# Moving a small weight preparation to GpSimd and its queue, and two requests to a later place

## The chip, the cores and the metric

The kernel runs on one core of one Trainium2 chip. A core has five engines that run their own instruction streams: TensorE (PE in the profile; its weight loads are PEld), VectorE (DVE), ScalarE (ACT), GpSimd (POOL) and SyncE (SP). All wait for one another by semaphores. Transfers between DRAM and the on-chip memory are requested by an engine and carried out by 16 DMA engines; a request from SP or ScalarE goes to a hardware queue of that engine, a request from GpSimd to a queue whose descriptors GpSimd writes. An engine issues its instructions in order, so an instruction that waits holds everything behind it on that engine.

The metric is the device time of one execution in microseconds, and the profile's span is the time from its first to its last instruction.

## The reference

Two independent sequences of 512 tokens and 1024 features go through the same two layers. All arithmetic is in float32; the kernel splits each operand into a high and a low part and multiplies these.

```python
def fourier_mix(h, w_out):
    B, S, _ = h.shape
    hg = h.astype(jnp.float32).reshape(B, S, N_FGROUPS, F_GROUP)
    f = jnp.fft.fft2(hg, axes=(1, 3), norm="ortho").real
    f = f.reshape(B, S, D_MODEL).astype(h.dtype)
    return f @ w_out

def trunk(x, ...):
    for i in range(DEPTH):
        j = i // N_MIXERS
        if i % N_MIXERS == 0:
            x = x + fourier_mix(rms_norm(x, fourier_norm[j]), fourier_w_out[j])
        else:
            x = x + gqa_attention(rms_norm(x, attn_norm[j]), ...)
        x = x + sq_relu_mlp(rms_norm(x, mlp_norm[i]), mlp_w_up[i], mlp_w_down[i])
    return rms_norm(x, final_norm)
```

Only the first operation, the Fourier mixing of layer 0, is touched by the change. The features fall into 8 groups of 128; the real part of a transform over 512 tokens and 128 features is taken per group, and the result is multiplied by the 1024x1024 matrix `w_out`.

## The kernel before, in words

**The work in order.** The kernel does the Fourier mixing of sequence 0 and then of sequence 1, then the first MLP for both, the attention, and the second MLP. The change lies in the first 60 us, in the mixing.

**The Fourier stage.** The real transform is symmetric, so each sequence is folded first: tokens are halved by sums and differences, and features too. `Front(q, c)` makes the folded inputs of sequence `q`, half `c`: squares for the norm (L124), the gain (L381), the difference `minus` (L394), the sum `plus` (L385) or, for sequence 1, `plus_there` (L390, an accumulating DMA from GpSimd), the norm's scale (L405, L411) and `combine` (L419 to L436). `transform(q, mid, hook)` multiplies by the token tables and then by the feature tables; for sequence 0 it uses exact tables (`exact`), for sequence 1 the tables `dcos`, `dsin`, `dalt` and `dfeat` (loaded by `table`, L309). `mid` and `hook0` are pieces of work that `transform` places between its products.

**The output weights.** `w_out` is folded as well. `Fold(j)`, for four row blocks, loads two halves from `w_four` on SP (L318, L319), takes their difference on VectorE (`minus`, L616) and their sum by an accumulating DMA that GpSimd issues (L617), and then splits both into high and low parts: `odd` from the difference, `even_hi` (L626, ScalarE) and `even_lo` (L630, VectorE) from the sum. `odd_outs` multiplies by the differences, for all eight output blocks at once, so that it holds all eight banks of the accumulator; `odd_put` (L696, L697) empties a bank on ScalarE into the output tile `xs[0, i]`. `even_outs` multiplies by the sums, one output block at a time, over four row blocks.

**The half-range rows.** Each feature group has one frequency, the 64th, that the folding does not cover. Its weight rows are eight differences of rows of `w_out`, and they enter as one more product at the end of each `even_outs` (L673): the weight tile there has 72 partitions, in which rows 0 to 7 and 64 to 71 hold the high part and rows 32 to 39 the low part. `FoldNyq` prepares this. `load` brings the raw rows (64 KB, from `w_nyq`), spread over 128 partitions; `combine` takes a difference on VectorE (L647) and its rounded copy on ScalarE (L648); `put` takes the low part on VectorE (L652), stores both parts to a DRAM tile called `nyq` (L653) and reads them back in the layout of the 72 partitions (L655, three loads). The store and the loads are requested by SP. The loads wait for the store's landing.

**What sets the order.** Up to the end of this stage, the program order of every engine is written out by hand (`manual_schedule` with all five engines). In later stages TensorE's order is written by hand and that of most other work is chosen by a planner, from planned times. Tiles named `u` come from one pool of 38 buffers; a new tile takes a buffer that is free by then, and its first write waits for whatever last used the buffer.

The order around the change, before: SP requests the inputs of sequence 0 and the exact tables, then the norms' columns `gc` (L333), the weights of `Fold(0)` and `Fold(1)`, the raw half-range rows (L643), the weights of `Fold(2)` and `Fold(3)`, and the four inputs of sequence 1 (L299), then the store and the three loads of `nyq`. GpSimd issues the four weight sums, the two `plus_there` of sequence 1's first half, the four tables, a small multiply (L401) and a memset (L425) of `g0`'s `combine`, and then the two `plus_there` of the second half. `gc` is first read by `blocks.gain` (L206), in the MLP's preparation.

Of the kernel before, what the change touches and what calls it, by code (L numbers as in the profile page):

```python
# [12 lines left out]
F32 = mybir.dt.float32  # L13
# [6 lines left out]
P = 128  # L20
# [4 lines left out]
KC = D // P  # L25
# [19 lines left out]
def trunk_kernel(ctx, tc, x_in, xt_in, y_out, tables, rope, gfour, gcol, grow, gfin,  # L45
                 w_four, w_nyq, w_qkv, w_o, w_a22, w_up, w_row2, w_row4, w_sum2, w_sum4, w_down):
    nc = tc.nc
    ctx.enter_context(nc.allow_low_precision(reason="operands split into float32r halves"))

    cons = ctx.enter_context(tc.tile_pool(name="cons", bufs=1))  # L50
# [10 lines left out]
    def nm(s):  # L61
        n_[0] += 1
        return f"{s}_{n_[0]}"

    def slot(shape, dt):
        return act.tile(shape, dt, tag="u4", name=nm("u"))
# [7 lines left out]
    def ps():  # L74
        return psp.tile([P, 512], F32, tag="ps", name=nm("ps"))

    def f32(ap):
        return ap.bitcast(F32)
# [116 lines left out]
    class Blocks:  # L195
# [25 lines left out]
        def put(self, name, f):  # L221
            h = slot([P, 2, 512], F32R), slot([P, 2, 512], F32R)
            split(h[0], h[1], f)
            self.b.setdefault(name, []).append(h)
# [82 lines left out]
    def table(k):  # L307
        tabs[k] = slot([P, D], F32R)
        nc.gpsimd.dma_start(tabs[k][:, : tables[k].shape[-1]], tables[k])  # L309
# [12 lines left out]
    def begin():  # L322
        gr = slot([P, D], F32)
        nc.sync.dma_start(gr, gfour)
        load_x(0, 0, nc.scalar)
        load_x(0, 1)
        exact_table(4)
        for t in range(2, 4):
            load_x(0, t)
        exact_table(5)  # L330
        exact_table(6)
        gc = cons.tile([P, 4 * KC], F32, name="gc")
        nc.sync.dma_start(gc, gcol)  # L333
        return gr, gc

    one = small(1)
    nc.vector.memset(one[:, :1], 1.0)
# [206 lines left out]
    def idle(o, n):  # L544

        for _ in range(n):
            nc.tensor.matmul(o[:, :256], filler, filler.unsqueeze(1).broadcast_to([P, 2, P]), start=True, stop=True)
# [85 lines left out]
    class FoldNyq:  # L633
# [7 lines left out]
        def load(self):  # L641
            self.h = slot([P, 4, 64], F32R)
            nc.sync.dma_start(f32(self.h[:, 2:]), w_nyq)  # L643

        def combine(self):
            h, ab = self.h, f32(self.h[:, 2:])
            nc.vector.tensor_sub(ab[:, 0], ab[:, 0], ab[:, 1])  # L647
            nc.scalar.copy(h[:, 0], ab[:, 0])  # L648

        def put(self):  # L650
            h, ab = self.h, f32(self.h[:, 2:])
            nc.vector.tensor_sub(h[:, 1], ab[:, 0], f32(h[:, 0]))  # L652
            nc.sync.dma_start(self.d.rearrange("i a (b f) -> (a b) i f", b=16), f32(h[:, :2]))  # L653
            for r, i in ((0, 0), (32, 1), (64, 0)):
                nc.sync.dma_start(f32(self.w[r : r + 8]), self.d[i])  # L655

# [20 lines left out]
    def odd_outs(q, fos):  # L679
        return outs(q, fos, wo, 256, 256)  # L680
# [26 lines left out]

    ET = mybir.EngineType
    with tc.manual_schedule(engines={ET.PE, ET.Activation, ET.DVE, ET.Pool, ET.SP}):
        gr, gc = begin()  # L710
        nc.scalar.activation(one[:, :1], one[:, :1], AF.Sqrt)
        cosX = [exact[0][:, :258], exact[0][:, 514:772], exact[1][:, 256:514]]
        sinX = [exact[0][:, 258:514], exact[1][:, :256], exact[1][:, 514:770]]
        ftX, pickX = exact[2][:, :256], exact[2][:, 256:334]
        f0, f1, wn = Front(0, 0), Front(0, 1), FoldNyq()
        idle(ps(), 61)
        f0.squares(0)
        f0.gain(0)
        f0.minus(0)
        f0.plus(0)  # L720
        f0.squares(1)
        f0.gain(1)
        f0.chain(0, 6)
        f1.squares(0)
        f0.minus(1)
        f0.plus(1)
        f0.scale_both(0)
        f1.gain(0)
        f1.squares(1)
        f1.chain(1, 2)  # L730
        f0.scale_both(1)
        f1.minus(0)
        f1.gain(1)
        fold = [Fold(j) for j in range(2)]
        wn.load()

        def mid():
            f1.chain(0, 1)
            f1.plus(0)
            f1.chain(2, 6)  # L740
            f1.scale()
            f1.minus(1)
            f1.plus(1)
            f1.combine()
            put_nyq()
            wn.combine()
            fold[0].minus()
            fold.append(Fold(2))
            fold.append(Fold(3))
            for t in range(NT):  # L750
                load_x(1, t)
            wn.put()
        g0, g1 = [Front(1, c) for c in range(2)]

        def hook0(at, j):
            if at == "seq":
                if j == 0:
                    fold[1].minus()
                    fold[0].odd()
                elif j == 2:  # L760
                    fold[2].minus()
                    fold[1].odd()
                elif j == 3:
                    fold[3].minus()
                    fold[2].odd()
            elif j == 3:
                fold[3].odd()
                g0.squares(0)
                g0.gain(0)
                g0.minus(0)  # L770
                g0.plus_there(0)
                g0.squares(1)
                g0.gain(1)
                g0.minus(1)
                g0.plus_there(1)
                for k in range(4):
                    table(k)

        transform(0, mid, hook0)
        for i in range(4):  # L780
            xs[0, i] = slot([P, 2, 512], F32)
        o = odd_outs(0, range(KC))
        g0.chain(0, 2)
        fold[0].even_hi()
        fold[1].even_hi()
        g0.chain(2, 6)
        fold[0].even_lo()
        fold[1].even_lo()
        g0.scale(slice(0, 1))
        fold[2].even_hi()  # L790
        fold[2].even_lo()
        odd_put(0, 0, o[0])
        fold[3].even_hi()
        fold[3].even_lo()
        for fo in range(1, 4):
            odd_put(0, fo, o[fo])
        g0.scale(slice(1, 2))
        g1.gain(0)
        for fo in range(4, 6):
            odd_put(0, fo, o[fo])  # L800
        g0.combine()
        for fo in range(6, 8):
            odd_put(0, fo, o[fo])
        g1.minus(0)
        g1.plus_there(0)
        g0.split_even()
        g1.gain(1)
        g0.split_odd()

        def even(fo):  # L810
            even_put(0, fo, even_outs(0, [fo])[0])
            if fo % 2:
                add_input(0, fo // 2)

        g1.squares(0)
        even(0)
        g1.minus(1)
        g1.plus_there(1)
        g1.squares(1)
        even(1)  # L820
        even(2)
        g1.chain(0, 2)
        even(3)
        g1.chain(2, 6)
        even(4)
        g1.scale(slice(0, 1))
        even(5)
        g1.scale(slice(1, 2))
        even(6)
        g1.combine()  # L830
        g1.split_hi()
        even(7)
        g1.split_lo()

        put_away(0, 2)
        load_xs(1, xt_in[1])
        raws = [load_raw(w_up[0, 2 * p]) for p in range(4)]
        blocks = Blocks(0)

        def hook1(at, j):  # L840
            if at == "seq":
                if j < 3:
                    square(0, j)
            else:
                square(0, 3 + j)
                if j == 3:
                    square(0, 7)

        transform(1, hook=hook1)
        for fo in range(KC):  # L850
            e, = even_outs(1, [fo])
            even_add(1, fo, e)
            if fo < 4:
                for i in range(2 * fo, 2 * fo + 2):
                    blocks.gain(0, i)
                if fo != 2:
                    put_away(0, fo)
            if fo == 2:
                blocks.root(0)
            if fo == 3:  # L860
                blocks.spread(0)
            if 3 < fo:
                blocks.first(fo - 4)
            if 5 < fo:
                blocks.first_lo(fo - 6)
        rows = []

        def gain1(fo):
            blocks.gain(1, fo)
            if fo % 2:  # L870
                put_away(1, fo // 2)

        for fo in range(KC):
            odd_add(1, fo, odd_outs(1, [fo])[0])
            if fo == 7:
                rows.append(halves(raws[3]))
            if fo:
                square(1, fo - 1)
            if fo > 1:
                gain1(fo - 2)  # L880
            if fo < 2:
                rows.append(halves(raws[fo]))
            if 1 < fo < 4:
                blocks.first_lo(fo)
            if fo == 5:
                rows.append(halves(raws[2]))
        square(1, KC - 1)
        for fo in range(KC - 2, KC):
            gain1(fo)
# [494 lines left out]
    for which, sc in (("q", HD ** -0.5), ("k", 1.0)):  # L1384
        r = slot([P, 2, NT, HD], F32)
# [319 lines left out]
    with tc.manual_schedule(engines={ET.PE}):  # L1705
# [14 lines left out]
        for k, name in enumerate(("t2", "t3", "t4")):  # L1720
            h = heads_out.operand(name)
# [334 lines left out]
```

## Time and profile before

| | us |
|---|---|
| median of 3 runs | 1689.15 |
| the three runs | 1680.93, 1689.15, 1689.36 |
| the profiled execution | 1683.1 |
| its span | 1681.3 |
| TensorE busy in the span | 1664.4 |
| VectorE, ScalarE, GpSimd busy | 1259.3, 873.4, 385.3 |

How to read the rows that follow. A row of the timeline is: start, length, engine, line of the kernel, operation, tile written and tile read with their shapes, how many, and in brackets the idle time of the engine just before and what ended it. A row of a wait list is: engine and tile, the line that waited, who ended the wait, then total time, how often, longest. A row of the chain is start, length and what; the chain is followed backwards from the end of the kernel, at each step to the event that released it. A row of the DMA list is: tile written and read, the engine that issued, how many, KB of each, and the time from the request to the landing. A row of a stretch gives its busy time per engine, the clock granted to TensorE, the mean share of the 16 DMA engines and the rate. The name `ps` is an accumulator bank, `w` and `raw` are weight buffers.

### The profile page before, as it was taken

Reading aid. Unit: us, or ns where it says so; the run is one execution under the profiler, and the core shown is the slowest. Engines: PE = TensorE matmul, PEld = TensorE weight load, DVE = VectorE, ACT = ScalarE, POOL = GpSimd, SP = SyncE. Lnnn points to the kernel's source line nnn. Section 1 sums busy time; section 2 is a strip of 40 time slices with the busy share of each in tenths; the row PEclk is TensorE's granted clock in tenths of the full one; section 3 lists DMA queues with packets and bytes.
Section 4 is the critical chain, followed back from the end, with each engine's and each line's share of the span. In section 5 each row is a group of like instructions: output and inputs, shape, how many; then the busy total and the mean of one; then the engine's idle time right before and its main releaser. Section 6 shows DMA issues by size and latency. Waiting matters only on the chain.

```text
span 1681.3 us, 22281 instructions
## 1 busy us (share of the span) xinstructions
PE 1664.4 (99%) x7845; PEld 1386.3 (82%) x7845; DVE 1259.3 (75%) x1850; ACT 873.4 (52%) x1538; POOL 385.3 (23%) x357
## 2 busy tenths in 40 slices
PE   9999999999999999999999999999999999999998
PEld 8988888888888888788878888888888888888887
DVE  7779786557886869869888877777855487878865
ACT  6766454446342435446698854554544553433334
POOL 2321443221000001324544303004422220000002
PEclk9999999999999999999999999999999999999999
DMA  9842655449775757425501146334644696757532
GB/s 319 249 154 94 208 188 193 157 163 368 257 225 165 247 173 228 169 76 187 177 1 39 63 164 224 124 114 162 213 152 156 225 371 196 235 157 233 180 102 100
DMA packets 122239, 302.99 MB, mean 180 GB/s; under 512 B 12408, under 2 KB 13560, under 8 KB 122128
## 3 DMA queue, kind: packets, MB, share of 16 engines
q1 hardware_dynamic: 98896, 254.21, 43.5%
q0 software_dynamic: 8832, 20.89, 5.8%
q10 hardware_dynamic: 14400, 26.48, 4.2%
q8 instruction: 61, 1.00, 0.2%
q14 instruction: 50, 0.41, 0.1%
HBM read 218.11 MB, written 82.38 MB: 179 GB/s over the span
## 4 chain that ended last, share of the span: by engine, by line
PE 84%; DVE 7%; DMA 4%; ACT 3%; issue 2%; POOL 0%; SPq 0%; DVEq 0%; ACTq 0%; POOLq 0%
PE ps L914 67%; PE ps L81 5%; PE ps L82 5%; PE ps L83 5%; DMA nyq<-u 1%; DMA raw<-w_sum 1%; PE ps L1489 1%; DVE u L87 1%; DVE w L87 1%; ACT u L86 1%; ACT t L1481 1%; DVE u L1120 1%; DVE u L219 1%; DVE u L235 0%; PE ps L172 0%
## 5 line engine op out<-in xcount | busy, mean ns | idle before, releaser
L914 PE MATMUL ps<-u,w 128*128 128x512 f32 x4944 | 1131.7, 389 | 2.4 <-DVE w L87 1.5
L914 PEld LDWEIGHTS ps<-u,w 128*128 128x128 f32 x4944 | 926.3, 188 | 198.3 <-DVE w L87 2.7
L86 ACT CAST w<-raw 128x1024 fp32r<-128x1024 f32 (+1 forms) x216 | 213.7, 994 | 312.2 <-PE ps L914 236.9
L87 DVE TENSOR_TENSOR w<-raw,w 128x1024 fp32r<-128x1024 f32 (+1 forms) x216 | 252.0, 1171 | 76.9 <-ACT w L86 76.7
L86 ACT CAST u<-u 128x1024 fp32r<-128x1024 f32 x144 | 145.0, 1047 | 82.7 <-PE ps L914 37.8
L87 DVE TENSOR_TENSOR u<-u,u 128x1024 fp32r<-128x1024 f32 x144 | 172.9, 1227 | 18.6 <-ACT u L86 18.5
L914 PE MATMUL ps<-u,u 128*128 128x512 f32 x600 | 143.2, 389 | 0.0
L1120 DVE TENSOR_TENSOR u<-ps,u 128x512 f32<-128x512 f32 x160 | 109.3, 684 | 39.0 <-PE ps L914 36.5
L1149 POOL DMA_DIRECT2D raw<-w_sum x32 | 27.9, 873 | 468.7 <-DMA raw<-w_sum 161.6
L1030 POOL TENSOR_TENSOR u<-u 128x512 f32<-128x512 f32 x28 | 37.6, 1344 | 425.2 <-ACT u L927 425.2
L914 PEld LDWEIGHTS ps<-u,u 128*128 128x128 f32 x600 | 112.5, 188 | 24.0 <-ACT u L945 0.5
L81 PE MATMUL ps<-u,u 128*128 128x512 f32 (+2 forms) x340 | 128.8, 381 | 0.5 <-ACT t L1481 0.3
L82 PE MATMUL ps<-u,u 128*128 128x512 f32 (+2 forms) x340 | 124.3, 366 | 0.3 <-DVE u L87 0.3
L83 PE MATMUL ps<-u,u 128*128 128x512 f32 (+2 forms) x340 | 124.1, 365 | 0.0
L164 POOL TENSOR_TENSOR t<-t,t 128x512 f32<-128x512 f32 (+1 forms) x54 | 77.0, 1431 | 192.2 <-ACT t L160 191.5
L926 ACT ACTIVATE t<-t 128x512 f32<-128x512 f32 x64 | 40.5, 632 | 109.5 <-DVE t L999 96.0
L87 DVE TENSOR_TENSOR u<-ps,u 128x512 fp32r<-128x512 f32 (+3 forms) x112 | 68.4, 634 | 8.0 <-ACT u L86 7.4
L81 PEld LDWEIGHTS ps<-u,u 128*128 128x128 f32 x340 | 64.3, 189 | 10.2 <-ACT u L86 1.5
L83 PEld LDWEIGHTS ps<-u,u 128*128 128x128 f32 x340 | 64.2, 189 | 9.9
L82 PEld LDWEIGHTS ps<-u,u 128*128 128x128 f32 x340 | 64.4, 189 | 9.2 <-DVE u L87 1.4
L986 DVE TENSOR_TENSOR t<-ps,u 128x512 f32<-128x512 f32 x32 | 22.0, 686 | 61.4 <-PE ps L914 53.6
L1483 POOL TENSOR_SCALAR t<-t,s 128x512 f32<-128x512 f32 x64 | 47.2, 739 | 74.1 <-DVE s L1482 59.9
(258 smaller groups left out, 2017.2 us busy)
## 6 DMA issues: line engine op xcount, KB each, us to landing
raw<-w_up SPq DMA_DIRECT2D x80, 512.0 KB, 4.5
u<-spill_t SPq DMA_DIRECT2D x60, 512.0 KB, 7.0
raw<-w_sum SPq DMA_DIRECT2D x56, 512.0 KB, 4.9
u<-spill_b SPq DMA_DIRECT2D x45, 512.0 KB, 5.9
spill_t<-u SPq DMA_DIRECT2D x84, 256.0 KB, 2.0
spill_b<-t ACTq DMA_DIRECT2D x60, 256.0 KB, 4.4
raw<-w_row SPq DMA_DIRECT2D x28, 512.0 KB, 4.3
park<-u SPq DMA_DIRECT2D x24, 512.0 KB, 4.3
```

The costliest lines, as they stand in the source:

```text
L81: nc.tensor.matmul(out, lh, rh, start=first, stop=False)
L82: nc.tensor.matmul(out, lh, rl, start=False, stop=False)
L83: nc.tensor.matmul(out, ll, rh, start=False, stop=last)
L86: nc.scalar.copy(dst_hi, src)
L87: eng.tensor_sub(dst_lo, src, f32(dst_hi))
L164: nc.gpsimd.tensor_add(acc[q][:, :n], acc[q][:, :n], s[:, :n])
L914: nc.tensor.matmul(o, w[x][:, sl], h[k][y], start=first and k + i == 0, stop=k == n - 1 and i == 2, skip_group_check=not first)
L926: nc.scalar.activation(t, src, AF.Relu)
L1030: eng.tensor_sub(t[:, 0], b12, b11)
L1120: nc.vector.tensor_add(x, o, x)
L1149: nc.gpsimd.dma_start(s[:, 1], w[:, 3], accum_op=ALU.add)
L1483: nc.gpsimd.tensor_scalar(p, p, sm_[:, :1], 1.0, ALU.mult, ALU.mult)
```

## The change

The raw half-range rows are requested right after the tables of sequence 0. The three operations on them run on GpSimd, in `load`, and the store and the three loads are requested by GpSimd too. All of that precedes the four weight sums in GpSimd's order. `combine` and `put` of `FoldNyq` and their calls in `mid` are gone. The request for `gc` moves from before the weights to behind the inputs of sequence 1, at the end of `mid`. The four tables of sequence 1 are requested after `g0.combine()`, behind GpSimd's multiply and memset, where they stood ahead of these.

```diff
@@ begin()
         exact_table(5)
         exact_table(6)
-        gc = cons.tile([P, 4 * KC], F32, name="gc")
-        nc.sync.dma_start(gc, gcol)
-        return gr, gc
+        return gr
@@ class FoldNyq
         def load(self):
             self.h = slot([P, 4, 64], F32R)
             nc.sync.dma_start(f32(self.h[:, 2:]), w_nyq)
-
-        def combine(self):
             h, ab = self.h, f32(self.h[:, 2:])
-            nc.vector.tensor_sub(ab[:, 0], ab[:, 0], ab[:, 1])
-            nc.scalar.copy(h[:, 0], ab[:, 0])
-
-        def put(self):
-            h, ab = self.h, f32(self.h[:, 2:])
-            nc.vector.tensor_sub(h[:, 1], ab[:, 0], f32(h[:, 0]))
-            nc.sync.dma_start(self.d.rearrange("i a (b f) -> (a b) i f", b=16), f32(h[:, :2]))
+            nc.gpsimd.tensor_sub(ab[:, 0], ab[:, 0], ab[:, 1])
+            nc.gpsimd.tensor_copy(h[:, 0], ab[:, 0])
+            nc.gpsimd.tensor_sub(h[:, 1], ab[:, 0], f32(h[:, 0]))
+            nc.gpsimd.dma_start(self.d.rearrange("i a (b f) -> (a b) i f", b=16), f32(h[:, :2]))
             for r, i in ((0, 0), (32, 1), (64, 0)):
-                nc.sync.dma_start(f32(self.w[r : r + 8]), self.d[i])
+                nc.gpsimd.dma_start(f32(self.w[r : r + 8]), self.d[i])
@@
-        gr, gc = begin()
+        gr = begin()
+        gc = cons.tile([P, 4 * KC], F32, name="gc")
...
         f0, f1, wn = Front(0, 0), Front(0, 1), FoldNyq()
+        wn.load()
...
         fold = [Fold(j) for j in range(2)]
-        wn.load()
@@ mid()
             put_nyq()
-            wn.combine()
             fold[0].minus()
             fold.append(Fold(2))
             fold.append(Fold(3))
             for t in range(NT):
                 load_x(1, t)
-            wn.put()
+            nc.sync.dma_start(gc, gcol)
@@ hook0()
                 g0.plus_there(1)
-                for k in range(4):
-                    table(k)
@@ after the odd products
         g0.combine()
+        for k in range(4):
+            table(k)
```

## The prediction

> **What bounds the kernel now.** I read the page first, then the waits of TensorE, the chain of waits from 9 to 60 us, and the busy time by stretch.
>
> ```profile
> span 1681.3 us, 22281 instructions
> PE 1664.4 (99%) x7845; PEld 1386.3 (82%) x7845; DVE 1259.3 (75%) x1850; ACT 873.4 (52%) x1538; POOL 385.3 (23%) x357
> ```
>
> TensorE is the bound, with 16.9 us idle in the whole span. Only a gap of TensorE can be won. Its waits, longest first, give the gap, who ended it, how often, and the longest:
>
> ```profile
> PE ps L673 <- DMA u<-nyq: 2.3, 1, 2.3
> PE ps L914 <- DVE w L87: 1.5, 2, 1.4
> ...
> PE ps L81 <- ACT u L697: 0.9, 1, 0.9
> ...
> PE ps L83 <- DVE w L630: 0.6, 1, 0.6
> ```
>
> Three of these four lie within five microseconds of each other, and the chain (start, length, what) shows one cause behind them:
>
> ```profile
> 18.49 0.22 DVE u L647
> ...
> 20.00 21.27 DMA nyq<-u
> 42.04 4.63 DMA u<-nyq
> ...
> 46.92 0.36 PE ps L673
> ```
>
> The half-range rows are stored to DRAM by SP at 20.00 and land only at 41.3; then they are read back, and TensorE's first use of them, at 46.92, waits. The stretch that holds it has 2.35 us of TensorE in 5.90, the rest of the kernel 11.0 us of gaps in 1580:
>
> ```profile
> core 0: us, PE busy (x) PEld busy (x) DVE busy (x) ACT busy (x) POOL busy (x), PEclk, DMA share, GB/s
> 41.40:47.30 5.90, 2.35 (x15) 1.98 (x16) 4.32 (x8) 5.90 (x20) 0.87 (x3) 1.00 0.85 219
> 101.60:1681.30 1579.70, 1568.68 (x7164) 1297.23 (x7164) 1178.63 (x1695) 802.52 (x1390) 354.17 (x319) 1.00 0.52 175
> ```
>
> **The removed wait.** The timeline (start, length, instruction, idle before it and what ended that) ties the other two gaps to the same store:
>
> ```profile
> 41.35 0.37 ACT L696 COPY u<-ps 128x255 f32<-128x255 f32 x1 [2.97 <-DMA nyq<-u]
> 41.90 1.05 ACT L626 CAST w<-u 128x1024 fp32r<-128x1024 f32 x1
> 42.06 0.39 PE L81 MATMUL ps<-u,w 128*128 128x258 f32 x1 [0.93 <-ACT u L697]
> 42.98 1.23 DVE L630 TENSOR_TENSOR w<-u,w 128x1024 fp32r<-128x1024 f32 x1 [2.87 <-ACT w L626]
> 44.26 0.38 PE L83 MATMUL ps<-u,w 128*128 128x258 f32 x1 [0.61 <-DVE w L630]
> 46.92 0.36 PE L673 MATMUL ps<-u,u 72*128 72x258 f32 x1 [2.28 <-DMA u<-nyq]
> ```
>
> ScalarE's first `odd_put` writes a buffer that the store still reads; it stands 2.97 us, to 41.35, and the cast of the last weight sum, VectorE's low half and TensorE's bank follow late. Without the store there TensorE gets back 0.93 + 0.61 + 2.28 = 3.8 us, if nothing else is late next. Next in line is that last weight sum itself, below.
>
> **GpSimd's new work.** The rows and issue latencies (KB each, us to landing) that price it:
>
> ```profile
> 5.46 0.33 SPq L333 DMA_DIRECT2D gc<-gcol  x1
> ```
> ```profile
> raw<-w_four SPq DMA_DIRECT2D x3, 512.0 KB, 8.2
> raw<-w_four POOLq DMA_DIRECT2D x3, 512.0 KB, 11.0
> u<-dsin POOLq DMA_DIRECT2D x1, 512.0 KB, 5.3
> u<-w_nyq SPq DMA_DIRECT2D x1, 64.0 KB, 7.6
> ```
> ```profile
> 20.18 1.02 POOL L617 DMA_DIRECT2D raw<-w_four  x1 [17.73 <-DVE u L652]
> 28.91 0.89 POOL L617 DMA_DIRECT2D u<-w_four  x1 [3.80 <-DVE u L87]
> 39.97 0.55 POOL L309 DMA_DIRECT2D u<-dsin  x1 [1.97 <-issue]
> 41.97 0.20 POOL L401 TENSOR_TENSOR s<-s,mask 128x1 f32<-128x1 f32 x1
> ```
> ```profile
> L164 POOL TENSOR_TENSOR t<-t,t 128x512 f32<-128x512 f32 (+1 forms) x54 | 77.0, 1431 | 192.2 <-ACT t L160 191.5
> ```
>
> The load of the raw rows takes the place of the column norms on SP, 5.46, and with its old latency lands at 13.1. Three GpSimd operations of 128x64 lie between the 128x1 row (0.20) and the 128x512 row (1.43): in proportion 0.35 each, 14.1 when done. The store through GpSimd's queue has no row. The same queue's plain load took 5.3 us, its sums of 512 KB took 11.0, and SP's loads 8.2; I take 5.3, since it is GpSimd's own plain transfer, and the store is smaller: landed at 19.4. GpSimd stands in its order until then. It issues three loads at the 0.55 of the plain row (up to the 1.02 of the first sum): free at 21.1. Everything on GpSimd queues behind this; the first is the weights' sum of L617, formerly at 20.18, so it goes out 0.9 us late. The loads, read back in at most the 4.63 us of the chain, are in by 26, against a use at 43: hidden by 17 us.
>
> A late first sum delays the others, because the fourth went out at 28.91, just behind the first's landing. Times to landing of the first and of the fourth:
>
> ```profile
> DMA to landing us min/median/max: 8.5/8.5/8.5
> ...
> DMA to landing us min/median/max: 10.7/10.7/10.7
> ```
>
> (first sum, 20.18 + 8.5 = 28.7; fourth, 28.91 + 10.7 = 39.6.) With 0.9 us more the fourth lands at 40.5; cast 1.05 and low half 1.23 (rows above) end at 42.9. TensorE, ungapped from 41.4, wants the low half at 44.26 - 0.93 - 0.61 = 42.7. So it is 0.2 us late there, unless TensorE itself comes later.
>
> **Contention.** GpSimd's three operations fall at 13 to 14 us on VectorE's chain, which sets TensorE's start. Rows of VectorE alone, and beside GpSimd:
>
> ```profile
> 84.74 1.22 DVE L235 TENSOR_TENSOR u<-u,u 128x1024 fp32r<-128x1024 f32 x1
> 93.47 1.66 DVE L235 TENSOR_TENSOR u<-u,u 128x1024 fp32r<-128x1024 f32 x1
> ```
> ```profile
> 92.56 1.49 POOL L164 TENSOR_TENSOR t<-t,t 128x512 f32<-128x512 f32 x1 [18.33 <-ACT t L160]
> ```
>
> 0.44 us lost in 1.66 beside GpSimd makes 0.27 of GpSimd's time, 0.3 us for 1.05; at best nothing is lost. TensorE comes later by it, and with that the 0.2 us above are covered. The Trainium skill, in "SBUF — State Buffer", section "Who interferes with whom", says that a VectorE operation with two SBUF inputs and a GpSimd one that reads SBUF exclude each other for a whole instruction; by that the full 1.05 us would go and the gain would be 2.7 us. The row shows a partial loss, as two long operations that overlap in part can.
>
> **What else is removed or moved.** Rows of the readers and of what follows (the first column is the start):
>
> ```profile
> 55.12 0.69 DVE L702 TENSOR_TENSOR u<-ps,u 128x510 f32<-128x510 f32 x1 [0.20 <-PE ps L673]
> 56.68 0.69 DVE L702 TENSOR_TENSOR u<-ps,u 128x510 f32<-128x510 f32 x1 [0.87 <-PE ps L673]
> 60.03 0.69 DVE L450 TENSOR_TENSOR u<-t,u 128x512 fp32r<-128x512 f32 x1
> 58.03 0.28 PE L81 MATMUL ps<-u,ny 128*40 128x258 f32 x1
> 61.95 0.28 PE L83 MATMUL ps<-u,u 128*128 128x256 f32 x1
> 71.50 0.72 ACT L206 ACTIVATE u<-u,gc 128x512 f32<-128x512 f32 x1
> ```
>
> VectorE's two small subtractions (0.22 each) lie before the first weight difference, and ScalarE's copy was a wait on them; TensorE waits for neither: nothing won. The column norms go behind eight weight and four input loads on SP; they land no later than the old tail of that queue, 41.3, and are first read at 71.50: hidden by 30 us. The tables go behind a 0.20 us multiply and a memset, so their first request slips by 0.4 us; the next, at 39.97, came right after the fourth sum's landing at 39.6, and follows that. Three requests of 0.55 and a latency of 5.3 from there make 46.9 for the last; they are first read by TensorE at 58.03, 54.5 after the change: hidden by 7 us, by 3 if the sums are four later.
>
> **Does the gain last?** VectorE's chain to sequence 1 follows the last weight sum: its low half ends 1.3 us earlier (44.2 to 42.9), it loses its waits on TensorE (0.20 and 0.87), and its last split at 60.72 had 1.2 us before TensorE read it at 61.95. That is 3.6 us of lead against TensorE's 3.5: just enough.
>
> **Sum.** 3.8 for the three gaps, less 0.3 of contention, 0 for all that is hidden: 3.5 us. The profiled execution took 1683.1 us, its span 1681.3 and 1.8 around it; that becomes 1679.6. The median of the three runs, 1689.15, lies 6.0 above the profiled one; on it the forecast is 1685.6. A measurement of this kernel hardly tells 0.5% (8.4 us), the spread of those three runs, from no change; the likeliest case is 0.2%. Its own range is 1677 to 1689: the runs' 1680.9 less 3.5, and 1689.4 less the 0.6 of the second rival.
>
> **Rivals.**
> 1. *GpSimd blocks on its own store* (the other side). Beyond the 0.9 us, each microsecond by which the first sum slips is one that the fourth sum, and with it VectorE's chain, takes from TensorE. A store of 8.8 us (5.3 + 3.5) uses up the gain; from there the change is slower. At the 11.0 us of the sums it is 2.2 us slower, 1691; with 1.02 us per load, 3.6. For it: three of GpSimd's sums, issued while the queues were full, had that latency. Against it: they are eight times the store's size and add to what is there. Chance 0.09.
> 2. *The store waits in the common backlog*, whichever queue sends it: SP's 8.2 us at that time, 0.6 us of gain left, 1688.5. For it: everything SP issued then took that long. Against it: GpSimd's first sum, issued at 20.18, landed at 28.7, SP's store of the same moment at 41.3, so GpSimd's queue passes SP's. Chance 0.07. (The Trainium skill, "DMA: Bandwidth & Descriptors", section "Issuing engines are not separate DMA queues", says that DMAs of all issuers interleave on the same engines and that another issuer mostly saves issue time. The two landings disagree.)
> 3. *The spread of the runs sits in this wait.* 8.2 us lie between 1680.9 and 1689.2; a store of 21 us in a full queue could be what varies. Then its removal brings the runs to the fast value less 3.5: 1677. The profile, one execution, says nothing for it. Chance 0.18.
> 4. *The planner.* Behind the opening, other engines than TensorE are ordered from planned times, which change. Single waits there are 1.4 us at most now (L914), against 11.0 us of gaps in all; a new order can hardly win and might add some: two to eight such waits, 3 to 11 us, for 1685 to 1697. Chance 0.14.
> 5. *The change does nothing*: another arrival ends the same wait at 46.9, about 1689. Chance 0.04.
>
> The forecast keeps 0.48. Faster by over 0.5%: rival 3, and a sixth of the forecast for the spread of the runs, 0.26. Slower: half of rival 4, two fifths of rival 1, and 0.06 for the spread, 0.17. The rest, 0.57, is no change by that bound. The range reaches below rival 3's 1677 and to the upper part of rival 4, 1675 to 1695.
>
> **What will show it.** Right: the store issued by GpSimd near 14 us and landed before 21; no wait on `nyq` at L673, nor at L696 and L697; the first sum near 21; TensorE's stretch from 41.4 to the sequence-1 transform some 3.5 us shorter. Wrong: the first sum after 25; a wait for L630 of over 1 us; new waits on L914 after 100 us.

## The result, and the profile after

The changed kernel took 1681.62 us (median of 22 runs, 1679.25 to 1687.61), the kernel before on the same chip 1685.78 us (22 runs, 1680.93 to 1689.36). The ratio is 0.9977, with a 95% interval of 0.9969 to 0.9985: 3.9 us faster. The forecast was 1685.6 us, 3.5 us less than the median of 1689.15 known then; more runs put that median 3.4 us lower, so the difference was met and the absolute time lay 4.0 us too high.

The profiled execution took 1682.5 us, 0.6 less than the one before, with this head of the page:

```profile
span 1680.5 us, 22279 instructions
PE 1666.0 (99%) x7845; PEld 1387.7 (83%) x7845; DVE 1258.9 (75%) x1848; ACT 873.4 (52%) x1537; POOL 394.5 (23%) x364
```

A profile that gains 0.8 us of span beside a median that gains 4.2 has to be explained as well. First the waits of TensorE in the changed kernel (engine and tile, line, who ended the wait; total, times, longest):

```profile
PE ps L907 <- DVE w L87: 2.1, 2, 1.9
...
PE ps L473 <- ACT t L409: 1.0, 1, 1.0
...
PE ps L83 <- DVE w L628: 0.5, 1, 0.5
```

The 2.3 us on `nyq` are gone, and so are the 0.9 us at L81. GpSimd's timeline of the changed kernel (start, length, instruction, idle before it and what ended that) shows the whole new piece of work:

```profile
13.14 0.60 POOL L643 TENSOR_TENSOR u<-u 128x64 f32<-128x64 f32 x1 [10.70 <-DMA u<-w_nyq]
13.81 1.11 POOL L644 CAST u<-u 128x64 fp32r<-128x64 f32 x1
15.00 0.71 POOL L645 TENSOR_TENSOR u<-u 128x64 fp32r<-128x64 f32 x1
16.05 0.94 POOL L646 DMA_DIRECT2D nyq<-u  x1 [0.33 <-POOL u L645]
22.35 1.55 POOL L648 DMA_DIRECT2D u<-nyq  x3 [5.36 <-DMA nyq<-u]
23.89 2.75 POOL L615 DMA_DIRECT2D raw<-w_four  x3
33.53 0.86 POOL L615 DMA_DIRECT2D u<-w_four  x1 [6.89 <-DVE u L87]
```

The store is issued at 16.05 and has landed by 22.35, where the kernel before had 41.3. The three first weight sums go out together at 23.89; formerly the first left at 20.18. On TensorE's timeline the last weight sum's low half is a little late, and the product of half-range rows follows without a wait, at 43.55 instead of 46.92:

```profile
43.33 0.39 PE L83 MATMUL ps<-u,w 128*128 128x258 f32 x1 [0.50 <-DVE w L628]
43.55 0.35 PE L666 MATMUL ps<-u,u 72*128 72x258 f32 x1
54.68 0.28 PE L81 MATMUL ps<-u,ny 128*40 128x258 f32 x1
58.52 0.39 PE L83 MATMUL ps<-u,u 128*128 128x258 f32 x1
59.12 0.38 PE L83 MATMUL ps<-u,u 128*128 128x256 f32 x1
59.35 0.28 PE L468 MATMUL ps<-u,u 128*128 128x258 f32 x1
```

So TensorE is 3.37 us ahead there, 3.35 at the start of sequence 1's products (58.03 to 54.68), and 2.73 at the row of 59.35, which stood at 62.08: the two products of 58.52 and 59.12 came late, behind VectorE's splits. Most of this lead is lost much later, and not by a wait alone. The timeline's rows of TensorE there, before and after, and the stretches behind them, before and after (start and end, length, busy PE, PEld, DVE, ACT, POOL, then granted clock, DMA share and rate):

```profile
698.55 4.62 PE L914 MATMUL ps<-u,w 128*128 128x512 f32 x19 [1.38 <-DVE w L87]
```
```profile
696.46 6.90 PE L907 MATMUL ps<-u,w 128*128 128x512 f32 x22 [1.91 <-DVE w L87]
```

```profile
698.00:704.00 6.00, 5.45 (x24) 4.50 (x25) 3.75 (x6) 2.20 (x4) 3.23 (x3) 1.00 0.93 313
```
```profile
698.00:704.00 6.00, 6.00 (x21) 4.76 (x21) 1.69 (x3) 2.43 (x5) 5.06 (x4) 0.74 0.74 246
```

Behind a wait of 1.91 us, where the attention's weights `w_qkv` are being loaded, the granted clock averaged 0.74 over six microseconds, and the same 6 us held 21 products instead of 24. From 2.62 us of lead ahead of that wait (697.17 less 694.55, where the waits begin) and 2.09 behind it, 0.8 were left at the end of the span. Such drops turn out to be nearly half of the story.

### The profile page after: what moved, and what is told of

Read it like the earlier page. It is cut to its first block, busy times and chain, and to the rows that moved or that the text cites. A ratio compares the mean times of both kernels' runs of the same rounds, so it can differ in the third digit from the quotient of the medians.

```text
span 1680.5 us, 22279 instructions
## 1 busy us (share of the span) xinstructions
PE 1666.0 (99%) x7845; PEld 1387.7 (83%) x7845; DVE 1258.9 (75%) x1848; ACT 873.4 (52%) x1537; POOL 394.5 (23%) x364
## 4 chain that ended last, share of the span: by engine, by line
PE 87%; DVE 6%; ACT 3%; issue 2%; DMA 2%; POOL 0%; SPq 0%; DVEq 0%; ACTq 0%; POOLq 0%
PE ps L907 69%; PE ps L83 5%; PE ps L81 5%; PE ps L82 5%; PE ps L1482 1%; DVE w L87 1%; ACT t L1474 1%; ACT u L86 1%; DVE u L87 1%; DVE u L219 1%; DVE u L235 1%; DVE u L1113 0%; DMA u<-w_four 0%; DMA u<-x 0%; PE ps L172 0%
## 5 line engine op out<-in xcount | busy, mean ns | idle before, releaser
L907 PE MATMUL ps<-u,w 128*128 128x512 f32 x4944 | 1133.3, 390 | 2.9 <-DVE w L87 2.1
L907 PEld LDWEIGHTS ps<-u,w 128*128 128x128 f32 x4944 | 927.5, 188 | 199.1 <-DVE w L87 3.2
L907 PE MATMUL ps<-u,u 128*128 128x512 f32 x600 | 143.1, 389 | 0.1
L907 PEld LDWEIGHTS ps<-u,u 128*128 128x128 f32 x600 | 112.5, 188 | 23.8 <-ACT u L938 0.5
L81 PE MATMUL ps<-u,u 128*128 128x512 f32 (+2 forms) x340 | 128.8, 381 | 0.4 <-ACT t L1474 0.3
L83 PE MATMUL ps<-u,u 128*128 128x512 f32 (+2 forms) x340 | 124.4, 366 | 0.1
L919 ACT ACTIVATE t<-t 128x512 f32<-128x512 f32 x64 | 40.5, 632 | 109.8 <-DVE t L992 99.8
L83 PEld LDWEIGHTS ps<-u,u 128*128 128x128 f32 x340 | 64.2, 189 | 10.5 <-DVE u L448 0.5
L81 PEld LDWEIGHTS ps<-u,u 128*128 128x128 f32 x340 | 64.3, 189 | 10.1 <-ACT u L86 1.5
```

Of the source, the lines that this page charges most:

```text
L81: nc.tensor.matmul(out, lh, rh, start=first, stop=False)
L83: nc.tensor.matmul(out, ll, rh, start=False, stop=last)
L907: nc.tensor.matmul(o, w[x][:, sl], h[k][y], start=first and k + i == 0, stop=k == n - 1 and i == 2, skip_group_check=not first)
L919: nc.scalar.activation(t, src, AF.Relu)
```

## The experiments

All ratios are to the kernel before on the same chip, with 95% intervals. "Product" is the time at which TensorE starts the first product of half-range rows in the profiled execution (46.92 before, 43.55 after).

| kernel | ratio | product, us | wait for the read-back, us |
|---|---|---|---|
| changed kernel | 0.9977 [0.9969, 0.9985] | 43.55 | none |
| half-range rows on GpSimd alone | 0.9974 [0.9961, 0.9987] | 43.40 | none |
| the moves of `gc` and the tables alone | 0.9975 [0.9961, 0.9989] | 43.51 | none |
| move of the tables alone | 0.9977 [0.9966, 0.9988] | 44.40 | 1.1 |
| move of `gc` alone | 0.9999 [0.9987, 1.001] | 46.01 | 2.7 |
| rows formed in a place of their own | 1.0003 [0.9992, 1.0014] | 47.16 | 3.7 |
| changed, read-back by SP | 0.9973 [0.9963, 0.9982] | 43.24 | none |
| changed, rows left out | 0.9974 [0.9962, 0.9986] | 43.20 | none |
| changed, GpSimd longer | 0.9979 [0.9968, 0.9989] | 44.38 | none |
| before, wait filled | 0.9990 [0.9981, 0.9998] | 46.63 | 0.6 |
| changed, same filler | 0.9987 [0.9978, 0.9996] | 45.65 | none |

### Each half of the change alone

The kernel before with the half-range rows on GpSimd, `gc` and the tables where they were:

```diff
-            nc.vector.tensor_sub(ab[:, 0], ab[:, 0], ab[:, 1])
-            nc.scalar.copy(h[:, 0], ab[:, 0])
...
+            nc.gpsimd.tensor_sub(ab[:, 0], ab[:, 0], ab[:, 1])
+            nc.gpsimd.tensor_copy(h[:, 0], ab[:, 0])
+            nc.gpsimd.tensor_sub(h[:, 1], ab[:, 0], f32(h[:, 0]))
+            nc.gpsimd.dma_start(self.d.rearrange("i a (b f) -> (a b) i f", b=16), f32(h[:, :2]))
```

> Only the half-range rows' part of the change: GpSimd forms, stores and reads back; the norms' columns and sequence 1's tables stay where they were. Theory (the whole gain comes from the store leaving SP's queue): the time of the full change, 0.998 of the kernel before, with no wait on nyq, the first product of sequence 1's transform (ps<-u,ny) at 54.7 us within 0.5 against 58.03 before and 54.68 with the full change. Rival (the moves share in the gain, by taking requests out of the opening's traffic): at least 1 us later at that product than the full change, and a ratio of 0.999 or more.

And the kernel before with the two requests moved and everything else, the store by SP too, as it was:

```diff
-        nc.sync.dma_start(gc, gcol)
...
             wn.put()
+            nc.sync.dma_start(gc, gcol)
...
-                for k in range(4):
-                    table(k)
...
         g0.combine()
+        for k in range(4):
+            table(k)
```

> Only the two moves: the norms' columns behind the inputs of sequence 1, the tables behind g0's combine; the half-range rows as before. Theory: nothing, ratio 1.000 within 0.1%, the wait of 2.3 us on nyq at L673 still there, the first product of sequence 1 at 58.0 within 0.5. Rival (the moves share in the gain): 1 us or more earlier at that product.

Measured: 1680.84 and 1681.3 us against 1685.02, ratios 0.9974 and 0.9975. Each half has the whole gain, so the gains don't add. For the first half that was expected. For the moves it was not: they leave SP's store as late as it was, and yet TensorE doesn't wait. The rows of SP and TensorE in the kernel with the moves alone:

```profile
20.91 0.38 SPq L651 DMA_DIRECT2D nyq<-u  x1
40.24 1.02 SPq L653 DMA_DIRECT2D u<-nyq  x3
43.51 0.36 PE L671 MATMUL ps<-u,u 72*128 72x258 f32 x1
```

The store, 20.91, landed only just before the loads at 40.24. The third load was requested at 40.97, and by 43.51 the rows were there, in 2.5 us or less; before, the read-back's 4.63 us, counted from the third request too, ended at 46.7, and TensorE started at 46.92. The question became why it is faster.

### Which move, and by what

Three kernels, each the kernel before with a single edit. The tables alone:

```diff
                 g0.plus_there(1)
-                for k in range(4):
-                    table(k)
...
         g0.combine()
+        for k in range(4):
+            table(k)
```

> Kernel before with one edit: sequence 1's four tables are asked for behind the opening (where the change puts them), everything else as before. The two moves together took 4 us (1681.3 against 1685.0 us, ratio 0.9975), with the nyq store still on SP's queue. Theory: the tables are the whole of that, so this gives 0.9970 to 0.9982, the product of half-range rows (ps<-u,nyq) starts near 43.5 us without a wait for the read-back (46.9 before). Rival: gc's place on SP's queue is what counts; then this stands at 0.9995 to 1.0005 and the product still starts near 46.9.

`gc` alone:

```diff
-        nc.sync.dma_start(gc, gcol)
...
             wn.put()
+            nc.sync.dma_start(gc, gcol)
```

> Kernel before with one edit: the column norms (gc) are asked for behind sequence 1's input instead of behind the exact tables; the four tables stay. Theory (the tables are the whole): no change, 0.9992 to 1.0008, and the product of half-range rows still starts near 46.9 us behind a wait of about 2.3 us. Rival (gc counts): 0.997 to 0.998 and a start near 43.5 us.

And the half-range rows in a place of their own, so that the output tile can't get the buffer which the store reads; in the kernel with both moves that exchange of buffers had happened by itself, since a moved table is also a moved claim on the pool of buffers:

```diff
-            self.h = slot([P, 4, 64], F32R)
-            nc.sync.dma_start(f32(self.h[:, 2:]), w_nyq)
+            self.h = exact[1][:, 770:898].rearrange("p (k f) -> p k f", k=2).bitcast(F32R)
+            self.ab = exact[2][:, 846:974].rearrange("p (k f) -> p k f", k=2)
+            nc.sync.dma_start(self.ab, w_nyq)
```

> Kernel before with one edit: the half-range rows are formed in free columns of the exact tables' buffers, so sequence 1's first output tile no longer takes the buffer that the nyq store reads; store, read-back, tables and gc stay where they are. Tells apart why moving the tables helped. Theory A (the buffer): ScalarE's first copy (L694) no longer waits for the store, so the gaps at L81 and L83 (0.93 + 0.61 us) go; the store and its read-back are as late as before, so the product of half-range rows still waits for the read-back at about 46.9 us, and TensorE gains nothing from the two earlier gaps: 0.9992 to 1.0005. Theory B (the buffer is the whole): the read-back is also early enough, start near 43.5 us, 0.997 to 0.998. Under A the whole comes from the tables' traffic beside the read-back, which took 4.6 us beside four tables.

Measured: 0.9977, 0.9999 and 1.0003. The tables are the whole of the moves' gain, `gc` and the buffer are nothing. In the kernel with `gc` moved alone, the timeline's requests for the tables and TensorE's product, and then the chain's read-back (start, length, what):

```profile
37.89 0.90 POOL L309 DMA_DIRECT2D u<-dcos  x1
39.89 0.55 POOL L309 DMA_DIRECT2D u<-dsin  x1 [1.10 <-issue]
40.44 0.54 POOL L309 DMA_DIRECT2D u<-dalt  x1
...
46.01 0.36 PE L671 MATMUL ps<-u,u 72*128 72x258 f32 x1 [2.65 <-DMA u<-nyq]
```
```profile
40.52 5.40 DMA u<-nyq
```

The same in the kernel with the tables moved alone:

```profile
40.52 0.60 POOL L309 DMA_DIRECT2D u<-dcos  x1 [1.75 <-ACT u L697]
41.10 0.57 POOL L309 DMA_DIRECT2D u<-dsin  x1
...
44.40 0.36 PE L673 MATMUL ps<-u,u 72*128 72x258 f32 x1 [1.08 <-DMA u<-nyq]
```
```profile
40.69 3.46 DMA u<-nyq
```

In both the store landed within 0.2 us of the same time (39.8 and 39.9, by the issue of what follows it). With the first table's 387 KB requested 1.9 us ahead of the first of the three loads, and the second's 512 KB at about the same time as they, the last load took 5.40 us; with the first table requested behind two of the three it took 3.46. In the kernel with both moves, where the first table was requested at 40.77 and so stood as it does here, it took 2.5 or less; single executions differ by that much, and what makes the difference between these two isn't known. The two other kernels with the tables ahead of the loads have 5.64 (rows in their own place) and 5.47 (wait filled), so that four profiles with the tables ahead show 4.63 to 5.64 and the two with them behind 3.46 and less. The expectation of no wait at all was missed: 1.1 us of it stayed in this execution, though the time gained is the same within the intervals. That it is the transfers of the tables which slow the loads is read from these rows and the ratios; a load of the same size without a table's meaning wasn't tried.

The place of its own took away what it was to take away and won nothing. ScalarE's and TensorE's rows there:

```profile
39.51 0.37 ACT L697 COPY u<-ps 128x255 f32<-128x255 f32 x1 [0.25 <-PE ps L83]
47.16 0.55 PE L674 MATMUL ps<-u,u 72*128 72x258 f32 x1 [3.71 <-DMA u<-nyq]
```

The first `odd_put` starts at 39.51 behind TensorE, not behind the store; TensorE arrives earlier at the read-back and waits for it longer, 3.71 instead of 2.28. The two early gaps at L81 and L83 are only the part of one delay that TensorE met earlier. They also depend on the execution: in the kernel with `gc` moved, which has the old buffer, the store landed 1.5 us earlier than before, and the row of the same copy names TensorE as what it waited for.

### What GpSimd's blocking costs

In the first kernel the three loads are requested by SP behind the inputs, so that GpSimd never stands for the store:

```diff
-                nc.gpsimd.dma_start(f32(self.w[r : r + 8]), self.d[i])
+        def fetch(self):
+            for r, i in ((0, 0), (32, 1), (64, 0)):
+                nc.sync.dma_start(f32(self.w[r : r + 8]), self.d[i])
...
                 load_x(1, t)
+            wn.fetch()
             nc.sync.dma_start(gc, gcol)
```

> The full change, but the three loads of the rows are requested by SP behind sequence 1's inputs, so GpSimd no longer stands until its store has landed. The first weight sum goes out near 20.2 instead of 23.89. By the prediction's rule (each microsecond of slip costs one), the 2.8 us by which it slipped more than forecast come back: the first product of sequence 1 at about 52 us. Rival (the sums make up for a late start, since the fourth slipped only by 1.3 us where the first slipped by 3.7): it comes at 54.0 to 54.6, the half microsecond of L83's wait and some of VectorE's chain, ratio to the kernel before 0.997 to 0.998.

In the second the half-range rows aren't formed at all:

```diff
         def load(self):
-            self.h = slot([P, 4, 64], F32R)
-            nc.sync.dma_start(f32(self.h[:, 2:]), w_nyq)
...
-                nc.gpsimd.dma_start(f32(self.w[r : r + 8]), self.d[i])
+            pass
```

> The full change without the half-range rows: nothing of them is loaded, formed, stored or read back, and their weight tile stays zero, so their part is missing from the mixing's output; TensorE still multiplies by it. This is the upper limit of what any place of this work can give. Theory (what is left after the wait on nyq is the weight sums and VectorE's chain): no better than with the loads on SP by more than 0.5 us, first product of sequence 1 at 53.5 to 54.5. Rival (contention with VectorE and the added traffic still cost): 1 us or more better than that, and TensorE's first product of the opening (L473) earlier by 0.3.

The third makes GpSimd's part longer:

```diff
             nc.gpsimd.tensor_sub(h[:, 1], ab[:, 0], f32(h[:, 0]))
+            for _ in range(6):
+                nc.gpsimd.tensor_sub(h[:, 1], ab[:, 0], f32(h[:, 0]))
```

> The changed kernel with six more subtractions of 128x64 on GpSimd ahead of the nyq store, which write the same value again, to price GpSimd's blocking. At 0.71 us each they put the store at about 20.4 us, its landing at 26.5 and the first weight sum at about 28.1 us (23.9 in the changed kernel, 20.2 before). The prediction's rule (every us that the first sum slips costs one): 4.3 us more, so about 1.0001 against the kernel before (0.9977 + 0.0025). Rival (the sums run into one another and the fourth lands only about a third as much later): the fourth lands near 42.4 us instead of 40.9, and the kernel loses 0 to 1.5 us, 0.9977 to 0.9986. Also near the rival's end: the half-range rows must then land by 43 us, which they do.

Measured: 0.9973, 0.9974 and 0.9979, with the first sum at 20.97, 20.78 and 27.45 us (23.89 in the changed kernel). Between the earliest and the latest lie 6.7 us of GpSimd, and 0.0005 of the time, less than the intervals; the rule of one to one would ask for 0.004. (In its profile the longest one does reach the product 0.8 us later than the changed kernel, 44.38 against 43.55.) With the rows left out, sequence 1's first product starts at 54.23, with the loads on SP at 54.27 (54.68 in the changed kernel): where GpSimd doesn't stand for the store, the rest of the work costs TensorE nothing that shows there. Why the rule fails, the sums' landings tell: the timeline of GpSimd in the longer kernel, and the fourth sum in the DMA lists of the changed and the longer kernel:

```profile
16.44 3.30 POOL L647 TENSOR_TENSOR u<-u 128x64 fp32r<-128x64 f32 x6
20.07 0.94 POOL L648 DMA_DIRECT2D nyq<-u  x1 [0.33 <-POOL u L647]
25.91 1.54 POOL L650 DMA_DIRECT2D u<-nyq  x3 [4.90 <-DMA nyq<-u]
27.45 2.75 POOL L615 DMA_DIRECT2D raw<-w_four  x3
33.90 0.86 POOL L615 DMA_DIRECT2D u<-w_four  x1 [3.71 <-DVE u L87]
```
```profile
u<-w_four POOLq DMA_DIRECT2D x1, 512.0 KB, 7.4
```
```profile
u<-w_four POOLq DMA_DIRECT2D x1, 512.0 KB, 7.8
```

The first sum, requested at 20.18, 23.89 and 27.45, landed by the trace's events at 28.7, 33.3 and 33.6; the fourth, requested at 28.91, 33.53 and 33.90, landed at 39.6, 40.9 (33.53 + 7.4) and 41.7 (33.90 + 7.8). The fourth's request slips by 4.6 and 5.0 us, but the transfer needs 3.3 and 2.9 us less than the 10.7 it took before; why, no run shows. Of 7.3 us by which the first request slips, 2.1 reach the last landing, and the last is what VectorE's chain needs.

### Is a wait worth more than its length?

In the profiles with long waits for the read-back the products behind it were slow. The stretch from 47 to 52 us (busy PE, PEld, DVE, ACT, POOL, then granted clock) before (2.28 us of wait), with `gc` moved (2.65), and with the rows in their own place (3.71):

```profile
47.00:52.00 5.00, 5.00 (x42) 5.00 (x43) 4.56 (x8) 3.93 (x9) 0.90 (x1) 1.00 0.30 52
```
```profile
47.00:52.00 5.00, 5.00 (x31) 5.00 (x31) 4.61 (x8) 3.27 (x9) 1.64 (x3) 0.66 0.30 52
```
```profile
47.00:52.00 5.00, 4.84 (x22) 4.87 (x23) 3.61 (x5) 2.72 (x7) 1.40 (x3) 0.50 0.30 52
```

These are 42, 31 and 22 products in the same 5 us. To see what such a wait costs, products that nobody reads are put at its place, in the kernel before and in the changed one:

```diff
         if extra is not None:
+            if q == 0 and fos[0] == 0:
+                d = ps()[:, :n]
+                for _ in range(19):
+                    nc.tensor.matmul(d, lhs(ws[3][0], fos[0]), u[:, 0], start=True, stop=True)
             for i, fo in enumerate(fos):
```

> Kernel before with 19 products of 128x258 that nobody reads, put on TensorE right ahead of the product of half-range rows, in a bank of their own. At 0.12 us each they fill 2.3 us, the wait for the read-back (2.28 us in the profile). It asks whether the wait costs more than its length: after waits of 2.65 and 3.71 us at this place (kernels with the tables or the buffers otherwise) the granted clock stood at 0.66 and 0.50 for the 5 us behind them, while in the profile of the kernel before it stayed at 1.00. Theory (only the length of the wait counts): no change, 0.9996 to 1.0008, since the filler runs in time that was idle. Rival (in many executions the clock falls behind the wait, and a part of the gain is that): 0.9985 to 0.9994, and the clock between 47 and 52 us is 1.00.

> The changed kernel with the same 19 products at the same place, where it has no wait. Theory (only the length counts): the gap comes back as work, 2.3 us on top of the changed kernel's 0.9977: 0.9988 to 0.9994, with the small rest to 1.000 for the two gaps at L81 and L83. Rival (the start of sequence 1's transform isn't what sets the end, the gain comes from elsewhere): it stays at 0.9975 to 0.9982.

Measured: 1683.59 us and 1683.9 us (11 runs each) against 1685.39 (21 runs), ratios 0.9990 [0.9981, 0.9998] and 0.9987 [0.9978, 0.9996]. TensorE's rows and the stretch behind them, in the kernel before with the wait filled:

```profile
43.53 2.45 PE L675 MATMUL ps<-u,w 128*128 128x258 f32 x19
46.63 0.36 PE L677 MATMUL ps<-u,u 72*128 72x258 f32 x1 [0.64 <-DMA u<-nyq]
```
```profile
47.00:52.00 5.00, 5.00 (x43) 5.00 (x43) 4.97 (x9) 3.50 (x10) 1.45 (x2) 1.00 0.30 52
```

The read-back is nearly as late as it was (the product starts 0.3 us earlier in this execution), TensorE does 19 useless products, and the kernel is faster by 0.0010, 1.7 us. The interval leaves from 0.3 to 3.2 us for it. The mean granted clock over all runs says the same: 0.9977 and 0.9978 for the kernel before on its chips and for `gc` moved, 0.9974 for the place of its own; 0.9985 to 0.9988 for every kernel without the wait or with 1.1 us of it, and 0.9987 for the wait filled. A difference of 0.001 in the mean clock over 1680 us is 1.7 us of TensorE. In the changed kernel the same filler costs 0.0010 of the time, 1.7 us, against a length of 2.45 us (the ratio lies just below the range expected, and the interval allows that length), as it should where TensorE's stretch sets the end; the two ratios come from different chips.

What a fall is, finer cuts show. Within a trace the granted clock changes only at times that lie whole multiples of 3.413 us apart (4.77, 697.68 and 701.09 us in the changed kernel), and a fall is one such stretch at 0.50, or two with the rows in their own place. First the stretch ahead of the fall and the fall itself in the changed kernel, then the two stretches that share the wait of 2.28 us in the kernel before:

```profile
694.26:697.67 3.41, 1.50 (x7) 1.04 (x6) 3.38 (x5) 0.00 (x0) 0.00 (x0) 1.00 0.94 311
697.67:701.08 3.41, 3.41 (x9) 2.65 (x9) 2.02 (x4) 2.20 (x4) 2.48 (x2) 0.50 0.90 240
```
```profile
42.08:45.49 3.41, 1.96 (x12) 1.55 (x12) 2.51 (x4) 3.41 (x10) 0.23 (x2) 1.00 1.21 313
45.49:48.90 3.41, 1.98 (x16) 2.01 (x17) 3.01 (x7) 3.38 (x11) 0.57 (x1) 1.00 0.06 17
```

A fall of 3.41 us at half speed is 1.7 us of TensorE, as much as filling the wait saved. With the twelve profiles cut in this way, four stretches at full clock between the first and the last product held TensorE idle for 1.91 us or more, and behind these four the clock fell; the next held 1.48 us, and it didn't. The wait of 2.28 us was cut in two, with 1.45 and 1.43 us of idle time in its stretches, other gaps included; the shorter one of 1.91 us lay within one. The first change of the clock comes at 4.5 to 7.4 us in these executions, so the cuts fall elsewhere each time, and the same wait has a fall behind it in some executions only.

So the gain of 3.9 us has two parts: some 1.7 us of clock, by the mean clocks about one fall per execution more than without the wait, and the rest, some 2.2 us, of the delay itself. That the falls of the executions without a profile lie behind this wait is concluded from the filler, not seen. The profiled execution before was one in which the clock had not fallen; the profiled one after had a fall elsewhere, at 698 us. The fall took most of the lead; that is why the two spans differ by 0.8 us only.

## Why the prediction was right, and where not

**The removed wait: right in place and size, wrong in make-up.** The waits at L673 and L81 went, that at L83 stayed with 0.5 us, and TensorE stood 3.4 us ahead (forecast 3.5). But 0.93 + 0.61 at L81 and L83 were no gaps of their own: the place of its own took them away and won nothing. The sum came out since the three together are one delay of the read-back, 46.92 less the 43.2 that the kernel without the rows shows, 3.7 us. That the whole came out at 3.9 is luck in part: some 2.2 us of this delay reached the end, and the clock behind the wait, 1.7 us, was no term of the sum.

**GpSimd's operations: too cheap.** 0.35 us each by proportion; they measured 0.60, 1.11 (the cast) and 0.71, from 13.14 to 15.71 instead of 1.05 us in all. Six equal subtractions in a row took 3.30 us, 0.55 each, and in the kernel with the rows alone the first subtraction took 0.38. What sets these times no run shows; the proportion was near for the fastest of them only.

**The store: nearly right.** 5.3 us were taken, 6.0 measured (5.5 to 6.2 in four variants); it was issued at 16.05, not near 14, and landed at 22.05, not before 21. The loads took 5.8 us, more than the 4.63 called the most, and were still far ahead of their use. Against rival 2 the store passed SP's backlog, where the same 64 KB took 21.3 us. The rows:

```profile
nyq<-u SPq DMA_DIRECT2D x1, 64.0 KB, 21.3
```
```profile
nyq<-u POOLq DMA_DIRECT2D x1, 64.0 KB, 6.0
u<-nyq POOLq DMA_DIRECT2D x3, 32.0 KB, 5.8
```

**The first weight sum: 3.7 us late instead of 0.9, and it didn't matter.** The step of rival 1, that each further microsecond is one lost, failed: first sums 3.7 and 7.3 us late put the last one 1.3 and 2.1 us later, and the longer GpSimd cost nothing that the runs resolve. Had the rule held, the 2.8 us beyond 0.9 would have left 0.7 us of the gain: two errors, the price of GpSimd's work and the rule, cancelled, and that is luck. In the sum for the last weight sum's low half, 40.5 + 1.05 + 1.23 is 42.8, not 42.9; the product that reads it waited 0.5 us, not 0.2.

**Contention: right in size.** VectorE's rows beside GpSimd's in the changed kernel, where the same operations took 1.22 and 0.16 before:

```profile
13.48 1.34 DVE L379 TENSOR_TENSOR u<-u,u 128x1024 f32<-128x1024 f32 x1
14.75 0.20 DVE L135 TENSOR_SCALAR s<-s 128x2 f32<-128x2 f32 x1
```

0.16 us for 2.4 us of GpSimd, against the 0.3 allowed. The full exclusion that the Trainium skill states ("SBUF — State Buffer", section "Who interferes with whom") isn't in VectorE's rows here; whether GpSimd stood for VectorE they don't tell.

**What is moved: wrong.** "Hidden by 7 us" was true of the tables' readers, which don't wait in the changed kernel. What was missed is whom the tables delay: their transfers ran beside the read-back that TensorE waited for. Moving them alone gave 0.9977, the whole result. Moving `gc` is worth nothing, as forecast. In the changed kernel both causes are removed, and either would have done.

**Does the gain last: nearly.** VectorE's lead was called just enough; it was 0.6 us short (3.35 to 2.73 at 59.35).

**The rivals.** The planner (4) changed nothing: behind the opening every engine has the same order in both kernels. Its range was 1685 to 1697, but 3 us on top of 1685.6 make 1688.6. That the spread of the runs sits in this wait (3) failed: from lowest to highest it was 8.4 us before and is 8.4 us after. What the wait holds of it is the clock behind it, not the store's time, and 1.7 us in the median, not the whole distance from 1689 to 1681. That nothing changes (5) is outside the interval. A longer wait on L914, now L907, was named as a sign of being wrong. It came, 1.91 us with a fall of the clock against 1.38; with GpSimd longer it was 1.93 with a fall, and in the other nine profiles 0.35 to 1.48 without one. Whether the change lengthens it can't be told from single executions.

**Left open.** Whether the wait of 1.9 us that ends at 696.46 could be filled as well wasn't tried. One fall costs 1.7 us; how often the wait for the read-back brought one is known only from the mean clocks, and its price by the runs' times only as 0.3 to 3.2 us, since each profile shows one execution.

## What to carry to other kernels

When a transfer is late, list what else moves in its last microseconds: a transfer that is early for its own reader may be asked for later, and that alone may free the path. Two edits that remove two causes of the same wait don't add, so try each alone. And price a wait of TensorE of some 2 us or more above its length where the granted clock shows a fall behind it in some executions (here 1.7 us for each fall); useless products in the wait tell how much. A single profile without a fall says little of the other executions.

## What the runs showed of the hardware beyond that

- Waits of TensorE of 1.91, 1.93, 2.65 and 3.71 us were followed by a granted clock of 0.50 for 3.41 us, or 6.82 us behind the longest; one of 2.28 us was not (1.00). What told them apart in these runs was the idle time within one stretch of a grid of 3.413 us: the clock fell behind 1.91 us and more, and not behind 1.48. The Trainium skill, "TensorE: Matmul & The Clock Gate", section "Part 1: The HAM clock gate (the 'warmup' mystery)", tells of a window of 3.4 us that runs freely and is not started by the kernel; that a shorter wait has a fall behind it in one execution and a longer one has none in another agrees with it. The section "Why this matters for your kernels" asks for no gaps above about 3 us; here 1.91 us had a fall behind it.
- A cast of 128x64 took GpSimd 1.11 us, a two-input subtraction of that size 0.38 to 0.71.
- The last of four accumulating transfers of 512 KB landed 1.3 and 2.1 us later when the first was requested 3.7 and 7.3 us later.
